# Layer 0 of the context stream moved whole in front of the latent stream, in a two-layer attention and expert kernel

## The chip, the cores and the metric

The kernel runs on one core of a Trainium2 chip. The metric is the device time of one execution in microseconds (us). The engines are named as in the profile: PE multiplies matrices, DVE is the vector engine, ACT the scalar engine, POOL the GpSimd engine, SP the engine that issues most transfers. Each engine executes its own queue in order.

## The reference

There are two token streams: x, 512 latent tokens, and ctx, 256 context tokens, both 1024 wide. Layer 0 updates both; layer 1 updates x alone and needs of ctx only keys and values. Cut to what matters:

```python
for l in range(DEPTH):                     # DEPTH = 2, last = (l == 1)
    xn = modulate(rms_norm(h, norm1_g[l]), mod[:, 0], mod[:, 1])
    cn = modulate(rms_norm(hc, norm1_g[l]), mod_c[0], mod_c[1])
    ...
    o = blocked_diff_attn(q, jnp.concatenate([k, kc], axis=1), jnp.concatenate([v, vc], axis=1), lam)
    mix = mixer_output(o, p, ...)          # attention, pooling, convolution, gates, output projection
    if not last:
        oc = diff_attn_core(qc, kc, vc, lam)
        mix_c = mixer_output(oc, pc, ...)
        hc = hc + mod_c[2] * mix_c
    h = h + mod[:, 2] * mix
    h = h + mod[:, 5] * peer_ffn(xn2, peer_wq[l], peer_keys[l], peer_u[l], peer_v[l])
    if not last:
        hc = hc + mod_c[5] * peer_ffn(cn2, peer_wq[l], peer_keys[l], peer_u[l], peer_v[l])
```

`peer_ffn` searches, for each token and each of 8 heads, the 16 best of 16384 experts. An expert is one row of `peer_u` and one of `peer_v`; the output is the sum over the chosen experts of gate times gelu(u . x) times v.

## The kernel before

Matrices are float32. To multiply them, each operand is split into a high and a low part (`split`: ACT writes the high part, DVE the low one), and `mm3` runs three matmuls. `load_w` brings a weight half of 512 KB into `wraw` (three buffers) and splits it into `whi` and `wlo`. A matmul named `mm` has 512 columns for x and 256 for ctx; `qk` is the projection to q, k and v, always 256 columns; `sc`, `tr` and `po` are scores, transposes and output of the attention; `hid` and `dps` are hidden units and sums of the dense expert part.

The program is written layer by layer, but a scheduler with a time model of its own orders each engine's queue, by the order in the source as priority, which `prio` shifts. A layer of `trunk` is: norm; `qkv`, which stores q, k and v in HBM; `attend`, which reads them back head by head with DMAs issued on POOL (`hq`, `hk`, `hkl`, `hv`, two buffers each); `mixers`, whose letters name its steps (p pooling, c convolution, k convolution gates, g attention gate and merge of pooling, o convolution output, merge and output projection).

In layer 0 x and ctx go through `qkv` together, each weight being loaded once for both, then through `attend` (ctx's heads first, then x's). The other steps of ctx and x alternate as the scheduler finds room. Ctx's expert part (`ctx_ffn`) doesn't run over all experts: for each of its two tiles of 128 tokens, `gathered` fetches 128 rows of `peer_u` and 128 of `peer_v`, one expert row of 4 KB for each token at a time, with an indirect DMA on POOL into one of three buffers `row`. DVE multiplies a u row with x (`row<-row,gx`, L859), or adds a v row to the sum (`gacc<-row,gw,gacc`, L869). That makes 512 rows of 512 KB for ctx in layer 0, and 256 for the one tile of x that layer 1 gathers. They have the low priority 40000. At a tile's end the sum is transposed on PE, added to the residual and written to `hout`. X's other expert work (`ffn`) is dense: `keys` searches the best experts, `gates` builds gate matrices (`gps`), `hidden` computes `hid`, `values` sums `dps`.

Layer 1 begins with the norms of x and, from `hout`, of ctx, then `qkv` for both, then x's attention with pooling, convolution and convolution gates beside it.

## Time and profile before

| | |
|---|---|
| median of 3 runs | 5145.29 us (5134.71 to 5170.3) |
| the profiled execution | 5138.01 us |
| its span, first to last instruction | 5136.2 us |
| mean granted PE clock | 0.98 |

The profiled execution is one run of the program; its time is 1.8 us more than the span, which is what the windows and waits divide up. A window lists for each engine the busy time and, in brackets, the number of instructions that it started. A PE that is busy all the time is not always at its peak, because matmuls overlap; the number of matmuls in a window of equal work tells more. Idle time of an engine that nobody waits for costs nothing.

### The profile page before, as it was taken

Reading aid. Unit: us, or ns where it says so; the run is one execution under the profiler, and the core shown is the slowest. Engines: PE = TensorE matmul, PEld = TensorE weight load, DVE = VectorE, ACT = ScalarE, POOL = GpSimd, SP = SyncE. Lnnn points to the kernel's source line nnn. Section 1 sums busy time; section 2 is a strip of 40 time slices with the busy share of each in tenths; the row PEclk is TensorE's granted clock in tenths of the full one; section 3 lists DMA queues with packets and bytes.
Section 4 is the critical chain, followed back from the end, with each engine's and each line's share of the span. In section 5 each row is a group of like instructions: output and inputs, shape, how many; then the busy total and the mean of one; then the engine's idle time right before and its main releaser. Section 6 shows DMA issues by size and latency. Waiting matters only on the chain.

```text
span 5136.2 us, 73940 instructions
## 1 busy us (share of the span) xinstructions
PE 4934.7 (96%) x27373; PEld 4195.8 (82%) x27373; DVE 3946.9 (77%) x7993; ACT 1988.4 (39%) x2968; POOL 1180.5 (23%) x1028
## 2 busy tenths in 40 slices
PE   8999999998899999989999999999999999899999
PEld 5688787776688788768888789777679999899999
DVE  5457676697899998568888867666359999787885
ACT  4346664422333344222233234544334344332333
POOL 0001000024433343333333300000000434344320
PEclk9999999999999999999999999999999999999999
DMA  8667453468897889999999845533355888988995
GB/s 305 239 200 224 137 191 108 155 200 273 302 316 259 285 312 339 329 321 326 336 341 344 311 137 166 161 126 97 109 172 174 277 309 331 330 314 294 329 317 177
DMA packets 509035, 1280.77 MB, mean 249 GB/s; under 512 B 42496, under 2 KB 224640, under 8 KB 500352
## 3 DMA queue, kind: packets, MB, share of 16 engines
q1 hardware_dynamic: 302816, 669.35, 38.5%
q0 software_dynamic: 131968, 449.90, 25.7%
q10 hardware_dynamic: 73888, 156.79, 8.1%
q8 instruction: 215, 3.52, 0.3%
q14 instruction: 148, 1.21, 0.1%
HBM read 1098.13 MB, written 177.73 MB: 248 GB/s over the span
## 4 chain that ended last, share of the span: by engine, by line
PE 64%; DMA 14%; DVE 11%; issue 7%; POOL 2%; ACT 1%; SPq 0%; ACTq 0%; POOLq 0%; DVEq 0%
PE mm L98 6%; DMA row<-peer_v,ix 6%; PE mm L100 6%; PE mm L99 6%; DMA row<-peer_u,ix 6%; PE dps L99 5%; PE dps L100 5%; PE dps L98 5%; PE hid L100 4%; PE hid L98 4%; PE hid L99 4%; PE qk L98 3%; PE qk L100 3%; PE qk L99 2%; POOL row L846 2%
## 5 line engine op out<-in xcount | busy, mean ns | idle before, releaser
L100 PE MATMUL hid<-yh,ul 128*128 128x512 f32 (+1 forms) x2048 | 760.2, 372 | 33.9 <-DVE ul L94 33.6
L98 PE MATMUL hid<-yh,uh 128*128 128x512 f32 (+1 forms) x2048 | 757.1, 370 | 21.0 <-ACT yh L286 13.2
L846 POOL DMA_INDIRECT row<-peer_v,ix x384 | 568.5, 1480 | 876.7 <-DVE gacc L869 501.1
L846 POOL DMA_INDIRECT row<-peer_u,ix x384 | 521.4, 1358 | 1059.7 <-DVE row L859 617.7
L99 PE MATMUL hid<-yl,uh 128*128 128x512 f32 (+1 forms) x2048 | 755.7, 369 | 2.3 <-DVE yl L287 2.3
L98 PE MATMUL dps<-wh,vh 128*128 128x512 f32 (+1 forms) x2048 | 735.1, 365 | 20.0 <-ACT vh L93 18.6
L99 PE MATMUL dps<-wl,vh 128*128 128x512 f32 (+1 forms) x2048 | 741.7, 365 | 12.3 <-DVE wl L94 12.3
L100 PE MATMUL dps<-wh,vl 128*128 128x512 f32 (+1 forms) x2048 | 742.0, 364 | 10.4 <-DVE vl L94 10.4
L98 PE MATMUL mm<-hi,whi 128*128 128x512 f32 (+1 forms) x1856 | 666.5, 360 | 12.3 <-DVE y L582 3.1
L100 PE MATMUL mm<-hi,wlo 128*128 128x512 f32 (+1 forms) x1856 | 660.6, 358 | 14.0 <-DVE wlo L94 14.0
L99 PE MATMUL mm<-lo,whi 128*128 128x512 f32 (+1 forms) x1856 | 662.4, 357 | 3.5 <-DVE lo L94 3.5
L859 DVE SCALAR_TENSOR_TENSOR row<-row,gx 128x1024 f32<-128x1024 f32 x384 | 467.0, 1221 | 170.3 <-DMA row<-peer_u,ix 169.5
L869 DVE SCALAR_TENSOR_TENSOR gacc<-row,gw,gacc 128x1024 f32<-128x1024 f32 x381 | 488.1, 1281 | 133.7 <-DMA row<-peer_v,ix 132.6
L94 DVE TENSOR_TENSOR wlo<-wraw,whi 128x1024 fp32r<-128x1024 f32 (+1 forms) x356 | 427.2, 1202 | 179.6 <-ACT whi L93 177.2
L93 ACT ACTIVATE uh<-uraw 128x1024 fp32r<-128x1024 f32 x256 | 271.5, 1061 | 716.4 <-PE hid L99 651.9
L93 ACT ACTIVATE whi<-wraw 128x1024 fp32r<-128x1024 f32 (+1 forms) x356 | 370.5, 1043 | 404.4 <-PE mm L99 305.2
L93 ACT ACTIVATE vh<-vraw 128x1024 fp32r<-128x1024 f32 x256 | 270.2, 1058 | 641.9 <-PE dps L99 395.1
L100 PEld LDWEIGHTS hid<-yh,ul 128*128 128x128 f32 x2048 | 390.2, 191 | 82.9 <-DVE ul L94 44.6
L98 PEld LDWEIGHTS hid<-yh,uh 128*128 128x128 f32 x2048 | 391.1, 191 | 64.1 <-ACT yh L286 15.6
L98 PEld LDWEIGHTS dps<-wh,vh 128*128 128x128 f32 x2048 | 386.7, 189 | 61.9 <-ACT vh L93 19.4
L99 PEld LDWEIGHTS dps<-wl,vh 128*128 128x128 f32 x2048 | 387.1, 189 | 54.8 <-DVE wl L94 14.4
L100 PEld LDWEIGHTS dps<-wh,vl 128*128 128x128 f32 x2048 | 387.2, 189 | 51.5 <-DVE vl L94 11.1
(332 smaller groups left out, 9480.4 us busy)
## 6 DMA issues: line engine op xcount, KB each, us to landing
uraw<-uT SPq DMA_DIRECT2D x256, 512.0 KB, 5.7
vraw<-v SPq DMA_DIRECT2D x256, 512.0 KB, 6.8
wraw<-w_in SPq DMA_DIRECT2D x216, 512.0 KB, 4.4
gd<-gst ACTq DMA_DIRECT2D x28, 2048.0 KB, 10.7
mw<-w_mod SPq DMA_DIRECT2D x96, 512.0 KB, 7.0
wraw<-wq SPq DMA_DIRECT2D x80, 512.0 KB, 6.0
hidd<-ge ACTq DMA_DIRECT2D x128, 256.0 KB, 5.6
G<-gd SPq DMA_DIRECT2D x32, 1024.0 KB, 10.7
```

Of the source, the lines that this page charges most:

```text
L93: self.nc.scalar.activation(hi, src, AF.Copy)
L94: self.nc.vector.tensor_tensor(lo, src, hi.bitcast(F32), op=OP.subtract)
L98: mm(ps, lh, rh, start=start, stop=False)
L99: mm(ps, lh, rl, start=False, stop=False)
L100: mm(ps, ll, rh, start=False, stop=stop)
L846: nc.gpsimd.indirect_dma_start(out=r, out_offset=None, in_=a[t], in_offset=bass.IndirectOffsetOnAxis(ap=idx[:, s:s + 1], axis=0))
L859: nc.vector.scalar_tensor_tensor(out=r, in0=r, scalar=1.0, in1=x, op0=OP.mult, op1=OP.mult, accum_out=hid[:, k:k + 1])
L869: nc.vector.scalar_tensor_tensor(acc, r, w[:, k:k + 1], acc, op0=OP.mult, op1=OP.add)
```

## The change

- **Layer 0.** Ctx runs through all of its layer 0 first: norm, `qkv`, attention, mixers, norm, key search, and its gather is issued. Only then come x's `qkv`, attention and mixers. The `w_in` weights of q, k and v are therefore loaded and split twice. The modulation of layer 1 (`w_mod`, 24 MB) moves from the start to x's `qkv`.
- **Mixers.** `conv_out` is cut in two. Step v multiplies the convolution output with its gates; `merge` later reads back what the attention gate wrote (`md`), adds and splits. The order is pckvgo for ctx and pc|kvgo for x in layer 0.
- **Gather.** A tile of ctx ends with a store of its summed rows (`natc`), as they are. Transposes and residual are done in layer 1 (`gather_end`), where ctx is normed. The pools of the gather live from the program's start, and x's attention in layer 0 has five buffers `at` in place of six.
- **Layer 1.** X's norm, `qkv`, pooling and convolution come first; then step a (`begin`) finishes ctx, projects its keys and values (weights loaded once more) and starts the attention; convolution gates and output stand beside it.

```diff
-                self.head(l, ap_, pss, pt_, q, k, kl, v, h, s, nk)
-
-    def head(self, l, ap_, pss, pt_, q, k, kl, v, h, s, nk):
+                self.head(l, ap_, pss, pt_, q, k, kl, v, h, s, nk, s.nt + ahead)
+
+    def head(self, l, ap_, pss, pt_, q, k, kl, v, h, s, nk, na):
         nc, nq = self.nc, s.nt
...
-            at = ap_.tile([P, nk * P], F32, tag="a", name="at", bufs=6)
+            at = ap_.tile([P, nk * P], F32, tag="a", name="at", bufs=na)
...
-    def conv_out(self, l, s, pp, z, m, gates):
...
-            for c in range(4):
-                g = gates[2 * c:2 * c + 2] if gates else self.conv_gate(l, s, pp, zp, c, 3)
-                w = self.load_w(a["conv_out_w"][l, c], KT, 256)
-                for cb in range(2):
-                    j, t = 2 * c + cb, g[cb]
-                    q = zp.tile([P, s.n], F32, tag="cq", name="cq", bufs=3)
-                    nc.sync.dma_start(q, self.md[l][j * P:(j + 1) * P, s.o:s.o + s.n])
-                    nc.vector.tensor_tensor(t, self.proj_t(pp, self.sub(w, cb), [z])[0][0], t, op=OP.mult)
-                    nc.vector.tensor_tensor(t, t, q, op=OP.add)
...
+    def conv_out(self, l, s, pp, z, gates):
+
+        for c in range(4):
+            w = self.load_w(self.a["conv_out_w"][l, c], KT, 256)
+            for cb in range(2):
+                t = gates[2 * c + cb]
+                self.nc.vector.tensor_tensor(t, self.proj_t(pp, self.sub(w, cb), [z])[0][0], t, op=OP.mult)
+
+    def merge(self, l, s, m, gates):
+
...
+            for j, t in enumerate(gates):
+                q = zp.tile([P, s.n], F32, tag="cq", name="cq", bufs=3)
+                nc.sync.dma_start(q, self.md[l][j * P:(j + 1) * P, s.o:s.o + s.n])
+                nc.vector.tensor_tensor(t, t, q, op=OP.add)
+                self.split(m.h[:, j], m.l[:, j], t)
...
-    def gathered(self, l, tiles, gp, gq, nat, late):
...
+    def gathered(self, nat, idx, g, gp, late, end=None):
         nc, a = self.nc, self.a
...
+            if end is None:
+                nc.sync.dma_start(nat, acc)
+        if end is not None:
+            end(acc)
...
+    def gather_end(self, l, nat, c, n, i, gp, gq, h):
+
+        nc = self.nc
+        nc.sync.dma_start(h, self.hmid[l][:, c:c + n].rearrange("(k p) t -> p k t", p=P))
+        for t in range(n // P):
+            acc = gp.tile([P, D], F32, tag="gend", name="gend", bufs=1)
+            nc.sync.dma_start(acc, nat[t * P:(t + 1) * P, :])
+            self.gather_add(l, acc, i, gq, h[:, :, t * P:(t + 1) * P])
+
+    def gather_add(self, l, acc, i, gq, h):
+
+        tr = gq.tile([P, 4, P], F32, tag="gtr", name="gtr", bufs=1)
+        for k in range(KT):
+            self.nc.tensor.transpose(tr[:, k % 4], acc[:, k * P:(k + 1) * P], self.ident)
+            self.nc.vector.scalar_tensor_tensor(h[:, k], tr[:, k % 4], self.modT[l][:, 40 + k, i:i + 1], h[:, k], op0=OP.mult, op1=OP.add)
...
-            self.qkv(l, [X, Cx], "kqv")
-            if l == 0:
-                self.attend(l, ea, [(Cx, XT, CT), (X, 0, TT)], "right")
-                with ExitStack() as e2:
-                    hc = self.mixers(l, Cx, self.pool(e2, "fc", 2, PSUM), cp, "pcgo")
-                with ExitStack() as e2, self.prio(4000):
-                    self.pooling(l, [X], self.pool(e2, "fp", 2, PSUM))
-                ea.close()
-                ges = self.ctx_ffn(l, hc)
-                ec.close()
-                with ExitStack() as e2:
-                    hm = self.mixers(l, X, self.pool(e2, f"fl{l}", 3, PSUM), xp, "gco")
-            else:
-                ec.close()
-                self.attend(l, ea, [(X, 0, TT)], "right")
-                with ExitStack() as e2:
-                    hm = self.mixers(l, X, self.pool(e2, f"fl{l}", 2, PSUM), xp, "pck|go", ea)
...
+            self.load_norm(0, Cx, load(Cx), lambda: self.modulation(0, (0,), mp, pp))
+            self.load_norm(0, X, load(X), side="right")
+            with self.prio(500):
+                self.modulation(0, (1, 2), mp, pp)
...
+        self.qkv(0, [Cx], "kqv")
+        with ExitStack() as ea, ExitStack() as e2:
+            self.attend(0, ea, [(Cx, XT, CT)], "right")
+            hc = self.mixers(0, Cx, self.pool(e2, "fc", 2, PSUM), cp, "pckvgo")
+        self.ctx_ffn(0, hc, gpools)
+        ec.close()
+        with ExitStack() as e2:
+            mp, pp = self.pool(e2, "mod1"), self.pool(e2, "mod1p", 2, PSUM)
+            self.modulation(1, (0, 1, 2), mp, pp)
+            self.qkv(0, [X], "kqv", "right")
+        with ExitStack() as ea, ExitStack() as e2:
+            self.attend(0, ea, [(X, 0, TT)], "right", 1)
+            hm = self.mixers(0, X, self.pool(e2, "fl0", 2, PSUM), xp, "pc|kvgo", ea)
         return ges, e3, hm
 
...
+    def trunk1(self, X, Cx, ges, eh, h):
+
+
+        hsrc = self.hsrc = self.hout
+        e3, ea = ExitStack(), ExitStack()
+        self.wpool, self.wbufs = self.pool(e3, "wp1"), 3
+        xp = self.parts(e3, "xn1", X)
+        self.norm(1, X, h, self.a1, 0, "a10", side="right")
+        eh.close()
+        self.qkv(1, [X], "kqv")
+
+        def begin():
+            ges.close()
+            with ExitStack() as ec:
+                self.parts(ec, "xc1", Cx)
+                self.load_norm(1, Cx, lambda h, hp, es: self.gather_end(0, self.natc, NX, NC, 1, hp, self.pool(es, "gq", 1, PSUM), h))
+                self.qkv(1, [Cx], "kv")
+            self.attend(1, ea, [(X, 0, TT)], "right")
+
+        with ExitStack() as e2:
+            hm = self.mixers(1, X, self.pool(e2, "fl1", 2, PSUM), xp, "pcakv|go", ea, begin)
+        return e3, hm
+
...
+                elif c == "a":
+                    begin()
...
+                elif c == "v":
+                    self.conv_out(l, s, pp, z, gates)
                 else:
                     self.parts(es, f"m{l}{s.i}", m)
-                    self.conv_out(l, s, pp, z, m, gates)
+                    self.merge(l, s, m, gates)
```

Where the order moves instructions. The queue of DVE during x's attention in layer 0, before: the steps of the softmax (`mx`, `rcx`, `at`, `tl`), of ctx's convolution (`y`) and weight splits.

```order
L576 SCALAR_TENSOR_TENSOR y<-z,cols,y 128x256
L442 TENSOR_SCALAR rcx<-rcx,nlam_100 128x1
L432 TENSOR_REDUCE mx<-sc 128x1
L576 SCALAR_TENSOR_TENSOR y<-z,cols,y 128x256
L582 TENSOR_TENSOR y<-mm,y 128x256
L443 SCALAR_TENSOR_TENSOR at<-p,rcx,at 128x768
L438 RECIPROCAL rcx<-smx 128x1
L433 TENSOR_SCALAR mx<-mx 128x1
L94 TENSOR_TENSOR wlo<-wraw,whi 128x1024
L94 TENSOR_TENSOR tl<-tr_4853,th 128x512
```

The same queue and place now:

```order
L445 SCALAR_TENSOR_TENSOR at<-p,rcx,at 128x768
L440 RECIPROCAL rcx<-smx 128x1
L574 TENSOR_TENSOR z<-mm,z 128x512
L94 TENSOR_TENSOR wlo<-wraw,whi 128x1024
L872 SCALAR_TENSOR_TENSOR gacc<-row,gw,gacc 128x1024
L442 TENSOR_SCALAR at<-p,rcx 128x768
L434 TENSOR_REDUCE mx<-sc 128x1
L440 RECIPROCAL rcx<-smx 128x1
L577 SCALAR_TENSOR_TENSOR y<-z,cols,y 128x512
L872 SCALAR_TENSOR_TENSOR gacc<-row,gw,gacc 128x1024
L584 TENSOR_TENSOR y<-mm,y 128x512
L435 TENSOR_SCALAR mx<-mx 128x1
```

Sums of gathered rows (`gacc`) now stand between the softmax steps of x's heads; before, the first row instruction came after the last head. Over the program's stretches the 512 row instructions of ctx now lie so: 38 beside x's `qkv`, 177 between the first and the last step of x's attention, 102 from there to x's second norm, 103 to the first gate product, 92 to the first expert sum. Before: 89 from the attention's end to the second norm, 96, 145, and 182 beside the expert sums.

POOL's queue in x's attention, before: the loads of two heads.

```order
L413 DMA hv_5117<-vd_69 128x768
L408 DMA hk<-kd_65 128x1536
L406 DMA hq<-qd_63 128x2x512
L410 DMA hkl<-ld_67 128x768
L413 DMA hv_5322<-vd_69 128x768
L413 DMA hv_5323<-vd_69 128x768
L408 DMA hk<-kd_65 128x1536
L406 DMA hq<-qd_63 128x2x512
```

The same queue now:

```order
L850 DMA row<-peer_u,ix_6329 128x1024 x14
L415 DMA hv_11548<-vd_69 128x768
L415 DMA hv_11549<-vd_69 128x768
L850 DMA row<-peer_u,ix_6329 128x1024
L410 DMA hk<-kd_65 128x1536
L408 DMA hq<-qd_63 128x2x512
L412 DMA hkl<-ld_67 128x768
L850 DMA row<-peer_u,ix_6329 128x1024
L850 DMA row<-peer_v,ix_6329 128x1024 x13
```

The loads of a head now stand behind row fetches, and row fetches behind loads of a head that wait for a buffer.

PE's queue at ctx's second norm in layer 0 (`nps` the sum of squares, `ntr` transposes for the gather), before:

```order
L99 MATMUL mm<-lo,whi 128x512
L100 MATMUL mm<-hi,wlo 128x512
L98 MATMUL mm<-hi,whi 128x512
L99 MATMUL mm<-lo,whi 128x512
L293 MATMUL ntr<-ident,nfull 128x128 x2
L100 MATMUL mm<-hi,wlo 128x512
L98 MATMUL mm<-hi,whi 128x512
L99 MATMUL mm<-lo,whi 128x512
L293 MATMUL ntr<-ident,nfull 128x128 x2
L100 MATMUL mm<-hi,wlo 128x512
```

And now:

```order
L99 MATMUL mm<-lo,whi 128x256
L100 MATMUL mm<-hi,wlo 128x256
L277 MATMUL nps<-nsq,ones 128x256 x8
L295 MATMUL ntr<-ident,nfull 128x128 x16
L98 MATMUL mm<-hi,whi 128x256
L99 MATMUL mm<-lo,whi 128x256
L100 MATMUL mm<-hi,wlo 128x256
```

Before, x's matmuls of 512 columns stood between the norm's steps; now the norm is followed by its own transposes and by ctx's key search, of 256 columns.

## Rows read from the trace of the kernel before

The columns of the windows view are: the window, its length, busy us and number of instructions of PE, of weight loads, of DVE, of ACT and of POOL, PE's clock, the DMA engines' busy share, GB/s.

**Rows 1.** The page: span, and busy time of each engine.
```profile
span 5136.2 us, 73940 instructions
...
PE 4934.7 (96%) x27373; PEld 4195.8 (82%) x27373; DVE 3946.9 (77%) x7993; ACT 1988.4 (39%) x2968; POOL 1180.5 (23%) x1028
```

**Rows 2.** 64 us windows, columns as in the sentence above.
```profile
576.00:640.00 64.00, 58.52 (x248) 39.47 (x248) 40.40 (x91) 43.60 (x66) 2.82 (x5) 0.84 0.35 111
...
1792.00:1856.00 64.00, 63.08 (x395) 51.24 (x394) 61.51 (x122) 29.56 (x49) 26.25 (x11) 1.00 0.85 309
2240.00:2304.00 64.00, 50.46 (x207) 40.11 (x207) 45.26 (x67) 16.55 (x23) 22.62 (x18) 0.89 0.93 323
2368.00:2432.00 64.00, 64.00 (x284) 52.99 (x284) 58.04 (x79) 18.49 (x24) 26.73 (x17) 1.00 0.95 341
2944.00:3008.00 64.00, 57.60 (x221) 41.40 (x220) 42.74 (x64) 21.21 (x35) 3.48 (x1) 0.93 0.57 180
3072.00:3136.00 64.00, 64.00 (x552) 64.00 (x552) 45.90 (x134) 27.12 (x39) 0.00 (x0) 1.00 0.40 132
```

**Rows 3.** The windows view by stretches of the program, same columns.
```profile
0.00:468.00 468.00, 445.08 (x3029) 335.40 (x3029) 270.19 (x802) 205.35 (x358) 31.84 (x84) 0.98 0.72 243
468.00:886.00 418.00, 411.24 (x2290) 326.60 (x2291) 298.87 (x564) 240.59 (x370) 22.67 (x65) 0.98 0.48 153
...
1092.00:1327.00 235.00, 209.46 (x882) 167.12 (x881) 182.80 (x239) 61.46 (x75) 103.68 (x90) 0.98 0.83 281
1327.00:1699.00 372.00, 342.14 (x1853) 290.26 (x1852) 339.99 (x1010) 125.29 (x173) 126.34 (x104) 0.96 0.84 285
1699.00:2261.00 562.00, 551.84 (x3155) 450.07 (x3153) 454.50 (x724) 211.67 (x329) 211.40 (x135) 0.99 0.90 320
2261.00:2987.00 726.00, 708.60 (x3101) 584.59 (x3102) 616.38 (x825) 207.35 (x264) 253.66 (x190) 0.99 0.93 323
...
3219.00:3648.00 429.00, 426.04 (x1791) 314.83 (x1792) 277.20 (x489) 206.68 (x316) 20.47 (x72) 1.00 0.38 122
3648.00:3809.00 161.00, 156.03 (x610) 117.24 (x611) 65.94 (x86) 41.29 (x52) 0.00 (x0) 0.94 0.40 132
```

**Rows 4.** The windows view for the instructions of tile mm alone.
```profile
1092.00:1327.00 235.00, 209.28 (x881) 166.75 (x879) 17.54 (x25) 7.04 (x12) 0.98 0.83 281
3219.00:3648.00 429.00, 300.02 (x1200) 219.94 (x1200) 17.03 (x24) 18.98 (x32) 1.00 0.38 122
3648.00:3809.00 161.00, 138.20 (x576) 112.63 (x576) 10.79 (x15) 4.71 (x8) 0.94 0.40 132
```

**Rows 5.** Waits from 1092 to 1327 us: total us, times, longest us.
```profile
POOL row L846 <- DVE row L859: 61.4, 39, 3.9
...
DVE row L859 <- DMA row<-peer_u,ix: 30.0, 21, 2.9
...
PE mm L100 <- DVE wlo L94: 13.5, 9, 3.2
```

**Rows 6.** The instructions of tile row from 1092 to 1327 us.
```profile
L859 DVE SCALAR_TENSOR_TENSOR row<-row,gx x48: 1209/1224/1278, 1092.1 to 1317.5; 128x1024 f32<-128x1024 f32 x48
...
L846 POOL DMA_INDIRECT row<-peer_u,ix x45: 933/1145/1881, 1093.6 to 1311.4; - x45
...
L869 DVE SCALAR_TENSOR_TENSOR gacc<-row,gw,gacc x35: 1276/1283/1287, 1141.1 to 1326.3; 128x1024 f32<-128x1024 f32 x35
...
DMA to landing us min/median/max: 4.4/6.0/8.7
```

**Rows 7.** Timeline: x's second norm, layer 0: start us, us.
```profile
1326.67 4.77 PE L275 MATMUL nps<-nsq,ones 128*128 128x512 f32 x10
...
1349.06 0.50 PEld L98 LDWEIGHTS hid<-yh,uh 128*128 128x128 f32 x2 [9.08 <-ACT yh L286]
```

**Rows 8.** DVE instructions by form: busy us, mean ns of one, idle before.
```profile
L94 DVE TENSOR_TENSOR wlo<-wraw,whi 128x1024 fp32r<-128x1024 f32 x344 | 419.0, 1220 | 175.7 <-ACT whi L93 173.2 <-PE mm L100 0.3
...
L631 DVE FIND_INDEX8 ti<-tv,rsc 128x8 uint32<-128x128 f32 x160 | 46.4, 290 | 0.0
```

More of the change, by code (lines that the diff above doesn't have):

```diff
@@ L206, in lambdas, with rotary @@
         nc.vector.tensor_scalar(self.agc[l], self.cols[:, C_AG + l:C_AG + l + 1], 1.0 - lam_init, None, op0=OP.mult)
-    def rotary(self, l, pool):
+    def rotary(self, l, pool, turn):
         nc, a = self.nc, self.a
@@ L213, in rotary @@
         nc.sync.dma_start(rows, bass.AP(tensor=r.tensor, offset=r.offset + 384 * l, ap=[[0, P], [1, 2 * HD]]))
+        gains = [rows[:, off:off + HD] for off in (R_QG, R_KG)]
+        if not turn:
+            return None, None, gains
         cs = pool.tile([P, XT, 2, 32], F32, name="cs")
@@ L224, in rotary @@
                                                g[:, 1 - s][:, None].to_broadcast([P, XT, 32]), op0=OP.mult, op1=OP.mult)
-        gains = [rows[:, off:off + HD] for off in (R_QG, R_KG)]
         return rc, rs, gains
@@ L879, in load_norm @@
-    def load_norm(self, l, s, hsrc, between=None, side=None):
+        with self.prio(late):
+            x = gp.tile([P, D], F32, name="gx", bufs=1)
+            nc.sync.dma_start(x, nat)
+            acc = gp.tile([P, D], F32, name="gacc", bufs=1)
+            for h in range(8):
+                hid = gp.tile([P, 16], F32, name="ghid", bufs=2)
+                for k in range(16):
+                    r = fetch("peer_u", h * 16 + k)
+                    nc.vector.scalar_tensor_tensor(out=r, in0=r, scalar=1.0, in1=x, op0=OP.mult, op1=OP.mult,
+                                                   accum_out=hid[:, k:k + 1])
+                w = gp.tile([P, 16], F32, name="gw", bufs=2)
+                nc.scalar.activation(w, hid, AF.Gelu_apprx_tanh)
+                nc.vector.tensor_tensor(w, w, g[:, h * 16:h * 16 + 16], op=OP.mult)
+                for k in range(16):
+                    r = fetch("peer_v", h * 16 + k)
+                    if h == 0 and k == 0:
+                        nc.vector.tensor_scalar(acc, r, w[:, k:k + 1], None, op0=OP.mult)
+                    else:
+                        nc.vector.scalar_tensor_tensor(acc, r, w[:, k:k + 1], acc, op0=OP.mult, op1=OP.add)
+            if end is None:
+                nc.sync.dma_start(nat, acc)
@@ L880, in load_norm @@
+    def load_norm(self, l, s, load, between=None, side=None):
         with ExitStack() as es:
@@ L882, in load_norm @@
             h = hp.tile([P, KT, s.n], F32, name="h")
-            for k in range(KT):
-                self.nc.sync.dma_start(h[:, k], hsrc[k * P:(k + 1) * P, s.o:s.o + s.n])
+            load(h, hp, es)
             self.norm(l, s, h, self.a1, 0, f"a{l}{s.i}", between=between, side=side)
@@ L900, in run @@
         self.EC, self.stored = 2, 20
+        self.gath, self.late = (0, 1), (0, 40000)
         X, Cx = Stream(0, NX, 0), Stream(NX, NC, 1)
@@ L916, in parts, with trunk0 @@
         return p
[L918 removed]
+    def trunk0(self, X, Cx):
         a = self.a
[L923 to L969 removed]
@@ L971, in mixers, with load, f @@
-    def mixers(self, l, s, pp, xp, order, attn=None):
+        hsrc = self.hsrc = a["hT"]
+        e3, ec = ExitStack(), ExitStack()
+        self.wpool, self.wbufs, self.mbufs = self.pool(e3, "wp0"), 3, 8
+        xp = self.parts(e3, "xn0", X)
+        ges, gpools = self.gather_pools("c0")
+        cp = self.parts(ec, "xc0", Cx)
+        with ExitStack() as e2:
+            mp, pp = self.pool(e2, "mod0", side="right"), self.pool(e2, "mod0p", 2, PSUM, side="right")
+            def load(s):
+                def f(h, *_):
+                    for k in range(KT):
+                        self.nc.sync.dma_start(h[:, k], hsrc[k * P:(k + 1) * P, s.o:s.o + s.n])
+                return f
+            self.load_norm(0, Cx, load(Cx), lambda: self.modulation(0, (0,), mp, pp))
+            self.load_norm(0, X, load(X), side="right")
+            with self.prio(500):
+                self.modulation(0, (1, 2), mp, pp)
@@ new lines, in trunk0 @@
+        self.dump("xn0", X, Cx)
+        with ExitStack() as e2:
+            tmp = self.pool(e2, "lam", 2)
+            for i in range(DEPTH):
+                self.lambdas(i, tmp)
+        self.qkv(0, [Cx], "kqv")
[4 more added lines that the diff above has]
+        ec.close()
+        with ExitStack() as e2:
+            mp, pp = self.pool(e2, "mod1"), self.pool(e2, "mod1p", 2, PSUM)
+            self.modulation(1, (0, 1, 2), mp, pp)
+            self.qkv(0, [X], "kqv", "right")
@@ L973, in mixers @@
+    def mixers(self, l, s, pp, xp, order, attn=None, begin=None):
         z, m, gates = Stream(s.o, s.n, s.i), Stream(s.o, s.n, s.i), []
@@ L1013, in gather, with gather_out @@
         nc.vector.tensor_copy(gk, g)
-        dst = self.hout if l == 0 else self.out
-        self.gathered(l, [(rows, ix, gk, self.hmid[l][:, cols], i, dst[:, cols])], gp, gq, self.natd[l], late)
+        self.gathered(nat, ix, gk, gp, late, end)
+    def gather_out(self, gp, gq, acc, c):
+        col = lambda d: d[:, c].rearrange("(k p) t -> p k t", p=P)
+        h = gp.tile([P, KT, P], F32, tag="row", name="gres", bufs=3)
+        self.nc.sync.dma_start(h, col(self.hmid[DEPTH - 1]))
+        self.gather_add(DEPTH - 1, acc, 0, gq, h)
+        self.nc.sync.dma_start(col(self.out), h)
     def ranks(self, mp):
```

146 lines of the change are left out of this document (44 added, 102 removed).

## The prediction

> **What bounds the kernel now.** I read the page's engine sums first. PE is busy for 96% of the span [rows 1], so the kernel can only gain where PE waits or runs its matmuls further apart than it must. Busy time hides the second kind, so the next view is the 64 us windows, where matmuls can be counted. In the undisturbed ones PE starts 284 matmuls of 512 columns in 64 us, 0.225 us each, or 552 of mostly 256 columns, 0.116 us each [rows 2]. Against these prices I read the stretches [rows 3]. From 2261 to 2987 us, layer 0's expert sums, PE holds its price almost throughout, although gathered rows run beside it. Between 1092 and 1327 us it does not: 881 long matmuls [rows 4] are worth 199 us and took 235. That is the first stretch in which ctx's gathered rows run, and the waits say how they cost PE time [rows 5]. POOL waits 61.4 us for DVE to release a row buffer, DVE waits 30.0 us for rows of the first table to land, and PE waits for the weight splits that stand behind those rows in DVE's queue. The row view has 48 and 35 of the two DVE row instructions in that stretch [rows 6], so one row takes 235 / 83 = 2.8 us. A row needs a POOL issue of 1.1 us, 6.0 us to land and 1.22 or 1.28 us of DVE; three buffers in turn give (1.1 + 6.0 + 1.25) / 3 = 2.8 us too. This closed loop, not DVE's load (183 of 235 us busy), set the pace. Elsewhere rows are sparser: 96, 145 and 182 in the next three stretches of the order, 3.9 us or more apart, and PE loses little.
>
> **What the change moves.** PE's instructions stay the same; what changes is what stands beside what. Counting the new order, ctx's 512 row instructions on DVE now fall so: 38 beside x's projection in layer 0, 177 between the first and last matmul of x's attention, 102 from there to x's second norm, 103 in the key stretch, 92 in the gate stretch, none in the expert sums. On PE the attention stretch holds eight heads and 861 long matmuls, the next one 768.
>
> *X's attention.* Layer 1 shows the same work without rows: eight heads and 1200 long matmuls in 429 us [rows 3, 4]. 1200 x 0.225 = 270, so the heads cost 159 us. With 861 matmuls (194 us) the stretch would take 353 us. Its 177 rows at 2.8 us want 496 us, and DVE executes in order, so PE cannot leave them behind: **+143 us**.
>
> *From there to the second norm.* Layer 1 has it in 161 us with 576 matmuls (130 us), so 31 us of chains [rows 3, 4]. With 768 matmuls it is 173 + 31 = 204 us; 102 rows want 286: **+82 us**. The rows that lost 235 - 199 = 36 us between 1092 and 1327 are these same rows at their old place: **-36 us**.
>
> *POOL's queue.* The loads of q, k and v for x's eight heads used to stand ahead of all rows there; now rows stand between them, so a late row buffer delays a head. In the main sum this is inside the 2.8 us; it is a rival below.
>
> *Ctx alone in front.* Its second norm and keys lose the cover of x's matmuls. The norm's chain: x's own runs from its first sum at 1327 us to the first matmul behind it at 1349 [rows 7], 22 us at 512 columns; I take 15 for 256 (bounds 5 to 22). Keys: 32 searches of five DVE steps at 0.29 us and 16 splits at 1.22 us [rows 8] are 46 + 20 = 66 us of DVE beside 384 matmuls of 256 columns and 32 of scores, 48 us: +18. The attention gate's chain stands bare before (PE clock 0.84 and 248 matmuls in its window [rows 2]) and stays so: 0. The merge is now a step of its own that reads back what the gate wrote: +8 (0 to 16). Together **+41 us**.
>
> *Weights loaded twice.* 24 loads and splits more in layer 0 and 16 in layer 1, 40 x 1.22 = 49 us of DVE and 20 MB. In the first 468 us DVE is 58% busy and DMA 72% [rows 3], in layer 1's attention DVE 65%: hidden, 0 (up to +15 if that cover is gone). Layer 1's modulation weights move to x's projection: 24 MB there, with 12 MB of weights and 38 rows of 0.5 MB, are 55 MB in some 230 us, 240 GB/s, below the 323 GB/s that the stretch at 2261 us sustains [rows 3]: 0.
>
> *What is given back later.* The expert sums lose their rows. 3072 matmuls at 0.225 are 692 us of the 726; part of the rest is the start of the sums (PE 50 of 64 us at 2240 [rows 2]), which stays, so -12 (0 to -30). Sparser rows in the gate stretch: -8 (0 to -20). At the layer's end PE is busy 57.6 of 64 us while x's norm follows the sums and ctx waits for its rows' end [rows 2]; x's chain stays, ctx's goes behind x's projection: -8 (0 to -12). **-28 us**.
>
> *Layer 1.* Pooling, convolution and projection now precede the attention, which keeps 262 matmuls as filler: 159 + 59 = 218 us of PE. DVE's share is 277 us less 39 splits (48) and the steps of pooling and convolution, some 200: still PE's, but with two score buffers less forgiving: **+10 us** (-10 to +30).
>
> Sum: 143 + 82 - 36 + 41 - 28 + 10 = **+212 us**. The profiled execution took 5138.0 us, 1.8 more than its span; the median of the runs is 5145.3. On the median this gives **5357 us, +4.1%**.
>
> **A rule weighed against the rows.** In this stretch POOL's issue of a row takes 0.93 to 1.88 us [rows 6] while DVE is 78% busy with float32 operations [rows 3]; around 1792 us, beside the 16-bit gate products, it takes 26.25 / 11 = 2.4 us [rows 2]. The Trainium skill, SBUF — State Buffer, section "SBUF: two separate sides", says that GpSimd writes the descriptors of its own DMAs and is locked out while VectorE holds the port pair that both share, so that such a DMA waits for descriptors. By that rule rows beside a dense DVE stretch would come later than 2.8 us. The trace agrees at 1792 us at most, not at 1092.
>
> **Rivals.**
> - *Rows land ahead of their turn.* If the loop keeps up, the attention stretch takes its 353 us and the next its 204; the sum is -36 + 41 - 28 + 10 = -13 us, **5132 us**, and with the ctx chains covered some 50 us less. It decides if a row comes every 353 / 177 = 2.0 us. For it: a quick row lands in 4.4 us [rows 6], and DVE has idle time at 468 to 886 (299 of 418 us busy [rows 3]). Against it: even (0.93 + 4.4 + 1.25) / 3 = 2.2 us is too slow, and DVE's work alone exceeds 353 us, as the next point shows.
> - *Only DVE's own work binds.* Layer 1's attention keeps DVE 277 us busy [rows 3]; with some 15 splits fewer 257, and 177 x 1.25 = 221 for the rows: 478 us. The next stretch: 66 + 10 + 128 = 204, no more than PE's. The two give +125 in place of +225: **5257 us**. This is the lower end of the mechanism.
> - *Heads and rows hold each other in POOL's queue.* If each of eight heads also waits for one landing and one row turn (6.0 + 2.8 us), the sum grows by 70: **5427 us**.
> - *Issue is locked out.* POOL at 2.4 in place of 1.1 us adds 1.3 / 3 = 0.4 us to each of 279 rows, +120 us: **5477 us**.
>
> **How the numbers follow.** Main case 0.56 (5357), DVE alone 0.17 (5257), queue 0.10 (5427), lock-out 0.05 (5477), rows in time 0.12 (0.07 near 5132, 0.05 below 5094). The likeliest is 5357. The range leaves out the rows-in-time case: its low end is DVE alone with the lower bounds of the small terms (ctx -20, later -22), 5215; its high end is the lock-out, 5480. About 1%, some 51 us, is what a measurement of this kernel can tell from no change; the three runs spread over 0.7%. Faster 0.05, same 0.07, slower 0.88.
>
> **What would show it.** Right: x's attention in layer 0 takes near 500 us with DVE's waits for rows and POOL's for buffers as the long ones, PE's clock falling to 1.2 GHz in pieces; x's second norm starts near 1557 us (1327 + 189 + 41) where it started at 1327; the expert sums hold 284 matmuls in 64 us throughout. Wrong: rows closer than 2.2 us apart in the attention, or an attention stretch under 400 us. I would be wrong by size if the ctx part alone ran much longer than 550 us, or if layer 1's attention, short of filler, fell well below PE's price.

## The result, and the profile after

The changed kernel takes 5592.6 us (median of 4 runs, 5581.6 to 5616.5) beside 5144.5 for the kernel before (4 runs): a ratio of 1.087, 95% interval 1.082 to 1.092, so 448 us slower. The forecast was 5357, with 5480 as its upper end. The page has the same count of TensorE instructions as before, 195 us more of them busy, in a span that is 444 us longer [rows 1]:

```profile
span 5579.8 us, 74045 instructions
...
PE 5129.3 (92%) x27373; PEld 4287.0 (77%) x27373; DVE 4001.5 (72%) x8033; ACT 2003.6 (36%) x2983; POOL 1131.8 (20%) x1028
```

The windows view by stretches answers to [rows 3]. Up to 473 us ctx, with x's first norm; to 640 its second norm, keys and pick; to 861 x's projection; to 1391 x's eight heads, cut where the projection matmuls beside them end; to 1636 the way to x's second norm; to 1685 that norm. Then the expert sums, and layer 1: x's projection, pooling and convolution (to 3596), ctx's norm and projection (to 3791), heads (to 4106, cut again), the way to the second norm.

```profile
0.00:473.00 473.00, 421.87 (x2846) 348.49 (x2847) 274.41 (x643) 239.04 (x390) 29.19 (x90) 0.94 0.68 224
473.00:640.00 167.00, 113.38 (x749) 101.62 (x748) 135.55 (x582) 49.15 (x84) 21.57 (x17) 0.80 0.45 156
640.00:861.00 221.00, 219.19 (x1396) 160.20 (x1397) 150.53 (x355) 79.31 (x116) 35.37 (x53) 0.99 0.85 295
861.00:1152.00 291.00, 276.68 (x1124) 204.69 (x1122) 255.76 (x408) 122.58 (x182) 121.31 (x121) 0.97 0.78 263
1152.00:1391.00 239.00, 156.66 (x330) 83.23 (x329) 193.91 (x325) 59.02 (x106) 110.69 (x106) 0.50 0.76 240
1391.00:1636.00 245.00, 185.47 (x711) 138.67 (x710) 169.28 (x219) 56.63 (x72) 108.13 (x95) 0.84 0.82 283
1636.00:1685.00 49.00, 29.55 (x109) 19.75 (x107) 34.50 (x44) 12.64 (x17) 19.75 (x17) 0.82 0.92 323
...
2588.00:3291.00 703.00, 702.20 (x3097) 580.92 (x3096) 393.04 (x508) 204.37 (x254) 0.00 (x0) 1.00 0.58 189
3291.00:3596.00 305.00, 291.82 (x1884) 260.91 (x1883) 210.64 (x471) 126.36 (x178) 1.53 (x22) 0.98 0.47 151
3596.00:3791.00 195.00, 190.72 (x1042) 166.17 (x1041) 103.38 (x175) 80.19 (x108) 6.40 (x20) 0.98 0.46 146
3791.00:3880.00 89.00, 89.00 (x362) 64.44 (x362) 50.62 (x89) 36.46 (x54) 3.56 (x6) 1.00 0.40 135
3880.00:4106.00 226.00, 200.63 (x493) 112.37 (x492) 129.25 (x269) 76.37 (x151) 14.00 (x33) 0.61 0.24 72
4106.00:4237.00 131.00, 112.51 (x418) 80.95 (x417) 50.15 (x70) 33.71 (x45) 1.92 (x1) 0.86 0.38 123
```

Read the clock beside the busy time. A stretch less PE's busy time times its granted clock is what I call **lost** below, an estimate, since the ends of matmuls are modelled. At 1152 to 1391 it is 239 - 156.66 x 0.50 = 161 us, at 3880 to 4106 226 - 200.63 x 0.61 = 104. To x's second norm the changed kernel loses 76, 76, 4, 23, 161 and 89, together 429 us; from 3291 to 4237 us 19, 8, 0, 104 and 34, together 165. Before, the heads of layer 1 and the way behind them lost 3 and 14 [rows 3]. What the two worst stretches share shows in the same view of tile mm alone (the projection matmuls), which answers to [rows 4]:

```profile
861.00:1152.00 291.00, 214.13 (x861) 160.29 (x861) 15.33 (x22) 11.29 (x19) 0.97 0.78 263
1152.00:1391.00 239.00, 0.00 (x0) 0.00 (x0) 0.00 (x0) 0.00 (x0) 0.50 0.76 240
...
3880.00:4106.00 226.00, 0.00 (x0) 0.00 (x0) 0.20 (x1) 0.00 (x0) 0.61 0.24 72
```

All 861 stand beside the first four heads of layer 0; the other four are **bare**: no other matmul lies between their own. In layer 1 six of eight are: between the first score of one head and that of the next, 131 to 151 projection matmuls start in layer 1 before; now 128 and 134, and then five times 0. The waits at 1152 to 1391 us (total us, times, longest us) are those of a chain that goes around all engines, with the rows' closed loop beside it:

```profile
ACT th L93 <- PE tr L450: 105.7, 29, 7.1
POOL row L850 <- DVE row L862: 39.5, 29, 2.0
...
PE po L99 <- DVE tl L94: 29.5, 14, 4.2
...
PE sc L429 <- ACT p L438: 24.5, 12, 5.0
```

### The profile page after: what moved, and what is told of

Its sections match the earlier page's. It is cut to its first block, busy times and chain, and to the rows that moved or that the text cites. A ratio compares the mean times of both kernels' runs of the same rounds, so it can differ in the third digit from the quotient of the medians.

```text
span 5579.8 us, 74045 instructions
## 1 busy us (share of the span) xinstructions
PE 5129.3 (92%) x27373; PEld 4287.0 (77%) x27373; DVE 4001.5 (72%) x8033; ACT 2003.6 (36%) x2983; POOL 1131.8 (20%) x1028
## 4 chain that ended last, share of the span: by engine, by line
PE 61%; DMA 13%; DVE 10%; issue 9%; POOL 3%; ACT 2%; ACTq 0%; SPq 0%; POOLq 0%; DVEq 0%
PE dps L99 6%; PE dps L100 6%; DMA row<-peer_v,ix 6%; PE dps L98 6%; PE mm L98 6%; PE mm L99 6%; PE mm L100 6%; DMA row<-peer_u,ix 5%; PE hid L100 3%; PE hid L99 3%; PE hid L98 3%; POOL row L850 3%; PE qk L99 2%; PE qk L100 2%; PE qk L98 2%
## 5 line engine op out<-in xcount | busy, mean ns | idle before, releaser
L850 POOL DMA_INDIRECT row<-peer_v,ix x384 | 531.7, 1385 | 920.4 <-DVE gacc L872 465.9
L850 POOL DMA_INDIRECT row<-peer_u,ix x384 | 509.0, 1326 | 1003.5 <-DVE row L862 507.0
L94 DVE TENSOR_TENSOR wlo<-wraw,whi 128x1024 fp32r<-128x1024 f32 (+1 forms) x396 | 475.6, 1203 | 293.2 <-ACT whi L93 291.7
L93 ACT ACTIVATE whi<-wraw 128x1024 fp32r<-128x1024 f32 (+1 forms) x396 | 412.6, 1045 | 427.5 <-PE mm L99 294.5
L98 PEld LDWEIGHTS mm<-hi,whi 128*128 128x128 f32 x1856 | 362.6, 196 | 121.5 <-ACT hi L93 51.7
```

The costliest lines, as they stand in the source:

```text
L93: self.nc.scalar.activation(hi, src, AF.Copy)
L94: self.nc.vector.tensor_tensor(lo, src, hi.bitcast(F32), op=OP.subtract)
L98: mm(ps, lh, rh, start=start, stop=False)
L850: nc.gpsimd.indirect_dma_start(out=r, out_offset=None, in_=a[t], in_offset=bass.IndirectOffsetOnAxis(ap=idx[:, s:s + 1], axis=0))
```

## The experiments

Before was timed again beside each group, at 5144 to 5155 us, so differences between groups under some 15 us say nothing. "Norm" is the start of x's second norm in layer 0 (before 1327, changed 1636 us). It is a soft mark, since a norm starts with the first block that is ready. "Hid" is the first expert matmul behind that norm, before 1349 [rows 7], changed 1685, on the timeline:

```profile
1685.15 0.50 PEld L98 LDWEIGHTS hid<-yh,uh 128*128 128x128 f32 x2 [16.00 <-ACT yh L288]
```

From norm to hid the kernels take 14 to 49 us; from hid to layer 1 the six without rows all take 1572 or 1573, so hid is the firmer mark. The end of the program, behind layer 1's second norm, takes 1326 to 1358 us in the 18 profiled executions, and most edits change nothing there; differences of that size at the end are put down to no edit.

**Layer 1's order put back.**

```diff
-        self.qkv(1, [X], "kqv")           # ctx: in begin(), at "a"
+        self.parts(ec, "xc1", Cx); self.load_norm(1, Cx, ...); self.qkv(1, [X, Cx], "kqv")
-            hm = self.mixers(1, X, ..., "pcakv|go", ea, begin)
+            hm = self.mixers(1, X, ..., "pck|gvo", ea)
```

> The changed kernel, with layer 1 alone put back: ctx is finished right behind x's norm, both streams are projected together, and pooling, convolution and convolution gates stand behind the heads again, so that some 140 projection matmuls stand beside every head instead of 70 beside the second and none beside the other six. Layer 0, the rows and the weights stay as changed. Theory of the bare heads: the changed order burns the matmuls ahead of the heads, the six bare heads run at the 1.2 GHz level; undone, layer 1 from its first norm to its second comes back from 946 us to about 825 us, and the kernel from 5593 to about 5475 us (5465 to 5500). Theory of the rows (what the prediction rests on): layer 1 has no rows and only 10 us to give back, so about 5583 us, no change that a measurement could tell.

5463.5 us, 129 less. Layer 1 between its two norms of x takes 831 us instead of 946. Projection, heads and the way to the norm, same view:

```profile
3298.00:3537.00 239.00, 225.84 (x1795) 213.68 (x1793) 172.90 (x474) 108.78 (x166) 5.18 (x9) 0.96 0.46 148
3537.00:3967.00 430.00, 427.43 (x1791) 315.64 (x1792) 277.19 (x488) 206.55 (x316) 20.48 (x72) 1.00 0.38 123
3967.00:4129.00 162.00, 157.03 (x611) 117.83 (x612) 65.81 (x86) 41.19 (x52) 0.00 (x0) 0.93 0.39 129
```

Lost are 22, 3 and 16, 41 us, where the changed kernel loses 165; its full-speed work is the same (790 and 781 us). Layer 1's order alone is worth 129 us (115 between the two norms of the profiled executions), and no row plays a part in it: none runs in either stretch.

**The rows left out, in the new order and in the old.** In both, `for h in range(8)` of ctx's rows in layer 0 does not run.

> The changed kernel without the gathered rows of ctx in layer 0: their 512 fetches and row operations are left out and a zero sum is stored, so the output lacks that part. Theory of the rows: every row cost x's trunk 2.8 us of DVE order; x's second norm of layer 0 comes about 225 to 250 us earlier (1636 to about 1400 us), the sums and gates behind it are shorter by some 20 us too; the kernel ends near 5340 us (5320 to 5370). Theory of the bare heads: of the attention's 530 us about half of the overrun is due to heads without projection matmuls beside them and stays, as does layer 1's loss of 120 us; the second norm comes only 110 to 150 us earlier and the kernel ends near 5450 us (5420 to 5490).

> The kernel before without the gathered rows of ctx in layer 0 (fetches and row operations left out, a zero sum in their place, so the output lacks that part). It prices the rows at their old place, and with the changed kernel without rows (5353 us) the order by itself. From the prediction's terms: 36 us up to x's second norm and some 60 behind it: about 5045 us (5010 to 5090). The two orders without rows then differ by 5353 less 5045, some 310 us, of which layer 1 is 125: layer 0's order alone would cost 150 to 200 us where the prediction had 41. If instead the order of layer 0 is nearly free without rows, as the prediction had it, this kernel should come near 5190 us, no faster than before.

The changed kernel without rows: 5353.3 us, 239 less, norm at 1469, hid at 1483. Before without rows: 5039.3, 116 less than before beside it, norm at 1303, hid at 1318. So the rows cost a net 123 us by the change, and the two orders by themselves differ by 314: 165 to hid, nothing from there to layer 1, 127 between layer 1's norms (950 and 824 us), and 20 behind, no more than the end varies. For the first run, the reading that gives the bare heads half of the attention's overrun (5450) is out; that of the rows (5340) is near in the total, but its norm near 1400 came at 1469. The stretches up to the norm, changed order without rows:

```profile
0.00:468.00 468.00, 419.75 (x2844) 345.92 (x2844) 272.92 (x643) 230.73 (x383) 29.11 (x90) 0.94 0.69 226
468.00:640.00 172.00, 133.76 (x885) 115.27 (x885) 136.78 (x593) 54.95 (x94) 2.40 (x2) 0.86 0.47 159
640.00:826.00 186.00, 186.00 (x1214) 136.35 (x1213) 103.79 (x277) 70.95 (x103) 7.35 (x24) 1.00 0.69 230
826.00:1100.00 274.00, 273.35 (x1150) 203.64 (x1149) 180.40 (x312) 123.11 (x190) 11.68 (x38) 1.00 0.37 121
1100.00:1250.00 150.00, 129.02 (x352) 75.13 (x350) 79.16 (x156) 47.96 (x88) 7.48 (x21) 0.65 0.20 63
1250.00:1469.00 219.00, 201.38 (x803) 154.35 (x804) 76.06 (x95) 55.12 (x69) 1.91 (x1) 0.91 0.37 123
```

And the old order without rows, up to its norm:

```profile
0.00:466.00 466.00, 445.01 (x3029) 334.94 (x3029) 270.09 (x802) 205.26 (x358) 31.98 (x84) 0.97 0.73 243
466.00:894.00 428.00, 422.71 (x2292) 332.01 (x2293) 299.49 (x566) 240.70 (x370) 22.76 (x65) 0.94 0.47 150
894.00:1303.00 409.00, 403.92 (x1937) 331.15 (x1936) 252.99 (x699) 139.72 (x197) 5.36 (x27) 0.99 0.43 137
```

TensorE's full-speed work is 1236 and 1229 us, the same; lost are 73, 57, 0, 1, 66 and 36, 233 us, against 34, 31 and 9, 74. Of the 166 us between the two kernels' norms, 159 are TensorE's time that no other work fills any more.

**Useless matmuls beside layer 1's bare heads.** In two doses, ahead of each of the six transposed blocks of heads 2 to 7:

```diff
             tr = pt_.tile([P, nq * P], F32, tag="tr", name="tr2")
+            if l == 1 and h in range(2, 8):
+                for i in range(4):            # 8 in the second kernel
+                    nc.tensor.matmul(tr, k[:, i % 2, :P], q[:, i % 2], ...)
```

> The changed kernel with work added: in layer 1, beside each of heads 2 to 7, 24 matmuls of 128x512 whose result is overwritten unread (4 ahead of each of the 6 transposed blocks), 144 in all. At full clock such a matmul costs some 0.25 us of TensorE (65 us for 263 in this kernel at a granted clock of 1.00), at the 0.61 of these heads some 0.55 us. Theory of the bare heads, with the clock as the reason: the added work keeps the engine busy enough for the granted clock to rise; a head's own TensorE time falls from 34 to 22 us and 6 us are added, so a head takes 30 to 33 us instead of 38, and the kernel is 25 to 45 us FASTER with more work in it. If the heads are slow as a chain of waits and the clock is no cause: the added matmuls cost 144 times 0.25 to 0.55 us less what they find idle, so 10 to 60 us SLOWER. Theory of the rows: no part of it here; it says 0.

> As the one before with 48 such matmuls beside each of the six heads (8 ahead of each transposed block), 288 in all. If the granted clock rises: a head takes 22 us of its own and 12 us of added work, so TensorE is bound at 34 to 38 us a head, and the kernel stays within 25 us of the changed one, with a granted clock near 1.0 over the heads. If the clock does not rise: 288 times 0.55 us, some 100 to 150 us slower.

5590.2 and 5599.1 us: no change, and 6 us more. The bare stretch with 144 of them, windows view:

```profile
3880.00:4110.00 230.00, 197.38 (x622) 120.64 (x622) 123.64 (x262) 73.57 (x145) 13.76 (x33) 0.82 0.20 60
```

And with 288:

```profile
3885.00:4132.00 247.00, 219.86 (x777) 143.59 (x777) 129.92 (x268) 76.56 (x150) 14.23 (x33) 0.90 0.19 59
```

The granted clock rises from 0.61 to 0.82 and 0.90, and the heads take 230 and 247 us instead of 226. For 144 both readings missed: the clock does rise, as the first said, but no time is won. That does not make the low clock free. In the changed kernel's bare stretch TensorE has hardly a gap at the lower level; at the full one more matmuls pass:

```profile
3998.00:4070.00 72.00, 67.74 (x147) 37.25 (x146) 39.35 (x85) 24.03 (x48) 4.39 (x16) 0.50 0.18 53
4070.00:4087.00 17.00, 12.20 (x49) 7.19 (x48) 12.14 (x25) 6.90 (x14) 0.00 (x0) 1.00 0.32 106
```

Layer 0's bare heads in the changed kernel without rows show the same:

```profile
1110.00:1134.00 24.00, 23.25 (x92) 15.79 (x90) 18.41 (x32) 10.32 (x17) 0.00 (x0) 1.00 0.34 111
1175.00:1250.00 75.00, 60.48 (x133) 33.12 (x133) 33.07 (x67) 20.40 (x39) 1.54 (x11) 0.50 0.06 18
```

That is 2.0 and 1.8 matmuls a us at the low level, 2.9 and 3.8 at the full one, though not of the same parts of a head. The added matmuls raised the clock, but 144 of them are themselves 40 us of full-speed work (0.28 each) in the heads' own queue, on top of the heads' 122, and can have used up what the clock gave. What these heads would take at full clock with nothing added, the runs do not show; an estimate by the first dose is between 190 us (230 less 40) and 230. Bare heads thus lose by waiting in their chain of score, maximum, exponential, division, transpose and split, and by the lower clock at which they then run; how much by which is open. The Trainium skill, Perfetto Trace Analysis, section "Identifying the Most-Contended Engine", warns that matmul busy time is no good measure of how close TensorE is to its roofline; the trace agrees: busy for 89% of the 226 us, it did 122 us of full-speed work.

**Layer 1's heads filled, ctx's projection still apart.**

```diff
-            hm = self.mixers(1, X, ..., "pcakv|go", ea, begin)
+            hm = self.mixers(1, X, ..., "apckv|go", ea, begin)
```

> The changed kernel with ctx's part of layer 1 (its norm and own projection) taken up right behind x's projection, and so the heads emitted ahead of pooling, convolution and gates: some 150 matmuls stand beside each head again, while ctx keeps a projection of its own. Theory of the bare heads: nearly all of what putting layer 1's order back gave (130 us) comes back, less some 10 to 25 us for the projection of its own: 5470 to 5495 us. If it was the joint projection that mattered: near 5580.

5535.1 us, 58 less than the changed kernel and 72 more than with layer 1's order back: a miss by 40. x's projection, ctx's norm and projection, heads, the way to the norm:

```profile
3310.00:3514.00 204.00, 168.75 (x1340) 159.18 (x1338) 148.93 (x383) 85.22 (x125) 1.47 (x2) 0.92 0.52 166
3514.00:3603.00 89.00, 77.44 (x504) 70.03 (x503) 52.41 (x118) 39.93 (x61) 4.67 (x16) 0.88 0.61 195
3603.00:4067.00 464.00, 461.36 (x1935) 344.12 (x1935) 286.80 (x499) 217.10 (x324) 19.19 (x63) 0.99 0.33 105
4067.00:4197.00 130.00, 110.10 (x417) 79.54 (x416) 52.41 (x72) 34.05 (x46) 1.92 (x1) 0.88 0.45 146
```

The heads lose 7 us again instead of 104. But the stretches of x's projection and of ctx's norm and projection, which pooling and convolution covered in the changed kernel, now lose 49 and 21 (19 and 8 there); the longest of TensorE's waits in them is for ctx's sums (`gtr` for `natc`, 14.0 us in two waits). The same matmuls can cover one or the other; the joint projection needed no cover for ctx.

**More beside layer 0's heads, with the rows and without.** Half of the convolution's gates and output (192 matmuls) ahead of the bar, as far as the memory reached:

```diff
-            hm = self.mixers(0, X, ..., "pc|kvgo", ea)
+            hm = self.mixers(0, X, ..., "pcK|Lgo", ea)    # K: blocks 0, 1 of k and v; L: 2, 3
```

> The changed kernel with half of x's convolution gates and half of its output convolution (192 matmuls, some 48 us at 0.25 us) moved ahead in layer 0 so that they stand beside x's heads; the rest stays behind them. By the order some 3 heads are left bare instead of 4. Theory of the bare heads (TensorE's idle time beside them is lost): the 192 matmuls go into time that is lost now and are gone from behind the heads: 30 to 50 us faster, near 5550 us. Theory of the rows (VectorE's order with the rows binds the heads, with or without matmuls beside them): attention and what follows keep their sum; within 12 us of 5593.

> The changed kernel without rows (as in the earlier run: fetches and row operations of layer 0's ctx left out, zero sums), and with half of x's convolution gates and output convolution (192 matmuls, 48 us at 0.25 us) beside x's heads in layer 0. By the order one or two heads stay bare instead of three to four. Theory of the bare heads (TensorE's idle time beside them, 66 us in 1100 to 1250 without rows, is what they cost): 30 to 50 us under the 5353 us of the kernel without rows, x's second norm near 1430 us. If the chain behind the heads is what counts: within 10 us of 5353.

With rows 5551.6 us, 41 less; without 5304.6, 49 less than 5353: both as the bare heads' reading had it. The norm's start misleads here: without rows it comes at 1414 instead of 1469, with rows it stays at 1635. But hid comes 27 us earlier without rows (1456) and 25 earlier with them (1661). So more cover beside the heads helps with the rows as without them, by some 25 us in layer 0; the rest lies for the most part at the program's end (17 and 22 us of the profiled executions) and cannot be put down to the edit.

**Layer 0's order put back, both orders back, rows held.** In the first, ctx and x are projected, attended and mixed in layer 0 as before the change; the second adds layer 1's. Held means that the row numbers have a zero added that is made from the last block of x's trunk.

> The changed kernel with layer 0's order put back: both streams projected together, ctx's attention and then x's, pooling, convolution and the gates of x beside ctx's second norm, keys and pick; what stays of the change is that the sums of ctx's rows go to memory as rows and are added in layer 1, and layer 1's new order with its six bare heads. Theory of this study so far (layer 0's order with the rows in x's trunk costs some 310 us to x's second norm, of which some 25 are given back; the bare heads of layer 1 some 125): 5593 less 285, near 5300 us (5265 to 5325). If the deferred sums were the cost, or layer 1's loss came from layer 0's rows, the kernel would stay above 5400 us or fall to about 5170.

> The changed kernel with both layers' orders put back: what stays of the change is that the sums of ctx's rows go to memory as rows and are transposed and added at layer 1. If the two orders are the whole loss, as the runs so far have it (5277 with layer 0's back, less 125 for layer 1's): 5150 us, within 15 us of before. If the deferral of the sums costs by itself: above 5175.

> The changed kernel with the gathered rows held back: their row numbers are made to depend on the end of x's trunk in layer 0 (a zero made from its last block is added to them), so no row runs beside x's projection, attention and gates; all 512 run from x's second norm on, and reach into layer 1, where this order needs them only behind x's convolution. Theory of the rows in the trunk: x's second norm comes at the 1469 us of the kernel without rows (1636 as changed); the rows then cost what they cost behind the norm at their old place, some 50 us in gates and keys, little in the sums, and 10 to 30 us in layer 1 where the last of them now lie: 5353 plus 75, near 5430 us (5400 to 5460). If a row costs the same wherever it lies, the kernel stays near 5590.

> As the one before, and the rows held back until x's second norm: the only part of the rows' price that the deferral lets one save. Theory: without rows the norm comes at 1303 us instead of 1327; the rows that lay ahead of it go into gates and sums at about half that price: 5 to 25 us faster than the kernel with both orders back, 5130 to 5145, about 0.3% under before. Rival: the last rows now end behind layer 0's sums, and layer 1, which in this order needs ctx at once, waits for them: 5200 to 5400 us.

Layer 0's back: 5277.1 us, within the forecast of this study. Both back: 5169.0, a ratio of 1.0045 (1.0028 to 1.0061) to before; so the deferred sums seem to cost some 25 us by themselves, more than I allowed. Where they cost them is open: the profiled execution takes 47 us more than before's, and 31 of these lie at the program's end. Rows held in the changed order: 5511.3, 81 less, not 160: hid comes at 1491, 194 earlier, but the rows press on what follows: 50 us more from hid to layer 1, 97 more between layer 1's norms. At the end they share VectorE with x's projection in layer 1, one line of that kernel:

```profile
3147.00:3351.00 204.00, 119.41 (x737) 110.13 (x736) 161.72 (x300) 50.39 (x72) 84.71 (x70) 0.73 0.81 266
```

117 of these 204 us are lost. Held with both orders back: 5297.4, the rival's case, not mine; layer 1 stands until the last row is in, as TensorE's longest wait says:

```profile
PE gtr L907 <- DMA gend<-natc: 153.9, 2, 151.8
```

No kernel with its rows beats the one before.

**What opens the front of layer 0.** Four edits: ctx's pick emitted behind x's projection (with rows); and without rows: no pick, no pick and no search over the keys (these outputs are not formed), and x projected jointly with ctx.

> The changed kernel with ctx's pick of the rows in layer 0 emitted behind x's projection instead of ahead of it, so that VectorE takes x's first query and key tiles before it. Theory of the hole: at 576 to 640 us TensorE waits with x's projection because VectorE is in ctx's pick (25 us lost by clock and idle time in this stretch without rows, and 32 us in the 108 us before it); with pick behind, 25 to 45 us of it come back, near 5555 us. Rival: VectorE has the same work to do up to the heads, and pick then delays x's tiles later or the rows only come later: 0 to 15 us.

> The changed kernel without rows, and without ctx's pick in layer 0 (row numbers and weights are not formed; nothing reads them here). If VectorE's pick in front of x's first query and key tiles is what opens the hole at 576 to 640 us: 20 to 40 us under 5353 us, with x's first heads that much earlier. If VectorE is short of time there anyhow, or the hole has another cause: 0 to 12 us.

> As the one before, and without the top-16 search over ctx's keys in layer 0 (160 VectorE operations of some 0.24 us, about 40 us; the scores are computed and left unread). If VectorE's search holds up TensorE at 468 to 576 us: another 20 to 35 us less, near 5295 us. If ctx's second norm and key projection wait for their own chain (square, sum, reciprocal root, split): within 10 us of the one before.

> The changed kernel without rows, with x and ctx projected together in layer 0 as before the change, and all else in the changed order. Theory: ctx's chain (attention, gates, second norm, keys, pick) has no work of x beside it as long as x's projection waits in line behind it; with x projected in front, x's heads fill the gaps. The 57 us at 468 to 640 and some 20 of those in ctx's projection go, but by the order five of x's heads then have no projection matmul beside them, some 15 us each lost: net 20 to 60 us under 5353 us. If the split of the projection is not the cause: within 15 us of 5353, or above.

The moved pick made it 62 us **slower** (5654.9). The changed kernel from 576 us, while x is projected:

```profile
576.00:704.00 128.00, 92.67 (x585) 71.48 (x586) 98.04 (x282) 31.60 (x47) 26.93 (x24) 0.83 0.74 261
704.00:832.00 128.00, 126.19 (x841) 89.81 (x840) 83.67 (x205) 44.32 (x67) 14.70 (x23) 1.00 0.81 281
```

The one with the pick behind, same windows:

```profile
576.00:704.00 128.00, 128.00 (x798) 80.48 (x800) 59.84 (x159) 41.04 (x59) 1.05 (x2) 1.00 0.74 258
704.00:832.00 128.00, 70.68 (x510) 67.32 (x503) 107.04 (x366) 31.96 (x45) 37.46 (x37) 0.77 0.53 170
```

The hole did not close, it moved behind the matmuls that were free to run at once, and grew from 51 to 74 us. Without rows, leaving the pick out brings hid from 1483 to 1448 and the kernel to 5297.6 (56 less, more than expected); the search on top of it brings hid 18 us further but no time (5310.2; the 18 us are lost in layer 1 and behind it). The joint projection gives 5280.4, 73 less and more than expected: hid comes at 1419. So up to hid the split of the projection, the pick, the search and one or two of the bare heads are worth some 64, 35, 18 and 27 us of the 165, the search tried with the pick, the others alone; that they add up was not tried.

## Why the prediction was wrong in size

The direction was right, and the net price of the rows nearly (161 forecast, 140 measured); two terms were not. In us, forecast and measured, up to hid and from there (by the runs without rows and the two kernels):

| Term | Forecast | Measured |
|---|---|---|
| rows ahead of x's norm, new place | 143 + 82 | 202 (1685 less 1483): 35 in x's projection, 167 from the first head to hid |
| rows at their old place | -36 | -31 (1318 against 1349) |
| given back later | -28 | -31 (rows cost 34 from hid to layer 1, 65 before) |
| layer 0's order without rows | +41 | +165 |
| layer 1 | +10 | +127, and 20 behind |
| sum | 212 | 452 (448 by the medians, 444 by the profiled executions) |

*Ctx alone in front*, the step that failed in layer 0, counted only the chains of ctx that lose cover. The base of *X's attention* failed with it: "with 861 matmuls (194 us) the stretch would take 353 us" took 159 us for eight heads from layer 1, where some 150 matmuls stand beside each head. Without rows the stretch takes 424 us and the next one 219 instead of 204. With rows it is 824 us from the first head to hid (861 to 1685), against 804 by the forecast (496 + 286, and the norm's own 22 [rows 7]): nearly right, by two errors that cancel, own work 78 us too small (657 instead of 353 + 204 + 22) and rows 58 too dear (167 instead of 225). That x's projection would pay 35 us for its rows was in no term, so the net price of the rows is near by luck in part. "Weights loaded twice: 0" failed too: a projection apart costs 72 us in layer 1 and 64 in layer 0. In layer 1 little of it is the loads: TensorE's waits for weight splits in the two stretches of projection come to 8 us; the rest I put down to ctx's chain without cover.

*Layer 1*, +10, is the same mistake with no rows to hide it: I summed TensorE's work, 218 us for the heads and their 262 matmuls, and called it the bound. The stretch took 315 us (3791 to 4106). The prediction's own sign of an error by size, layer 1's attention "short of filler", is what came.

The markers: near 500 us of attention (530), PE's clock at 1.2 GHz (0.50 means that level throughout 1152 to 1391), the sums at their price (3097 instructions in 703 us, 282 in 64) came true; the norm at 1557 did not. Rows came 2.5 us apart in the bare heads (94 in 239 us) and 3.5 before them (84 in 291), around the 2.8 assumed. Of the rivals, rows in time is ruled out by the 167 us. DVE's work alone would have cost 125; DVE is busy for 88, 81 and 69% of the three stretches, so its load alone is not the bound. Why the loop was cheaper than 225 was not tried (I would say that rows lay partly in gaps that the bare heads leave anyhow). The lock-out is not seen at its 2.4 us: the median issue of a row takes 0.94 us at 1152 to 1391 us, with VectorE 81% busy, and 1.08 (u) and 1.21 us (v) at 861 to 1152, with VectorE 88% busy. So the trace shows no sign of the rule of the Trainium skill, SBUF — State Buffer, section "SBUF: two separate sides", in this loss.

## What to carry to other kernels

Where TensorE bounds a kernel, independent matmuls beside a chain are a stock that can be spent once: before moving work, count in the built order what stands beside each link of every chain, not only the sum of the engine's work. Price a stretch by its length less busy time times granted clock; a change that leaves the work alone and moves this number has its cost there. A gathered row is dear beside work that VectorE releases in order (here 202 us for the 317 rows ahead of hid, 34 for the 195 behind it), and holding it back only helps if what it meets later has room. Mark a stretch by the first work behind a norm, not by the norm's start.

## What was not expected of the hardware

The granted clock of the same heads went from 0.61 to 0.82 and 0.90 when 24 and 48 unread matmuls stood beside each, and their time from 226 to 230 and 247 us: raising the clock by unread work won nothing. The low clock need not be free for that: in one stretch of 72 us at the lower level TensorE was busy for 67.74.
